# Low weight parts of the third group's block products: a ScalarE negation and an accumulating DMA in place of a VectorE subtraction, for six loads of fourteen

## The chip, the cores and the metric

The kernel runs on one core of a Trainium2 chip. A core has TensorE (PE, matrix products; its weight loads are shown apart as PEld), VectorE (DVE), ScalarE (ACT), GpSimd (POOL) and SyncE (SP), all running side by side, each working through its own list of instructions in order. DMAs move data between main memory and the on-chip memory SBUF; here SP issues the plain loads and POOL the accumulating ones, which add what they read to what lies at the destination. Matrix products land in PSUM, from which DVE or ACT take them away ("eviction"). The metric is the device time in microseconds of the whole program; lower is better.

## The reference, cut to what matters

The program is an encoder with two layers. Each layer is half a feed-forward block, a mixer (gated linear attention and softmax attention in parallel), and another half feed-forward block, on 528 tokens (512 and 16 learned ones) of 1024 channels, all in float32:

```python
for l in range(DEPTH):
    h = h + 0.5 * swiglu(rmsnorm(h, norm_gains[l, 0]), ffn_w_gate[l, 0], ffn_w_up[l, 0], ffn_w_down[l, 0])
    h = h + mixer(rmsnorm(h, norm_gains[l, 1]), ...)
    h = h + 0.5 * swiglu(rmsnorm(h, norm_gains[l, 2]), ffn_w_gate[l, 1], ffn_w_up[l, 1], ffn_w_down[l, 1])

def swiglu(x, w_gate, w_up, w_down):
    return (jax.nn.silu(x @ w_gate) * (x @ w_up)) @ w_down
```

The hidden width of a feed-forward block is 2816. The change lies in the last product, `... @ w_down`, of the first feed-forward block of each layer.

## The kernel before

**Numbers in two parts.** TensorE reads its operands in a shortened form of float32. To keep the accuracy, every weight tile `w` and every activation is split in two: a high part `hi`, which is `w` rounded to that form, and a low part `lo = w - hi`. A product then takes three matmuls: hi with the activation's high part, hi with its low part, and lo with the high part, in this order, so the low weight part is read by the third matmul of each three.

**Block products.** The feed-forward blocks use a two by two block scheme with seven products in place of eight. A product named "1" to "7" uses a block of the weight matrix or a sum of blocks. Products 1, 2 and 4 use plain blocks (11, 12 and 22, from `DIRECT`), which SP loads into the pool `raw` of three buffers (pool `wraw`). Products 7, 6, 5 and 3 use sums (`s3`, `s2`, `s1`, `s4`), most of them made by accumulating DMAs on POOL (`add`, line 224).

**Groups and steps.** The 22 hidden tiles are taken as 11 pairs in three groups of 4, 4 and 3 pairs (`GROUPS`). After each group its part of the down projection follows: for the two halves of the output ("quads", dq 0 and 1) seven products each, so fourteen loads a group. For the third group they are 768 columns wide, for the others 1024 (`wide`). Only the blocks in `ALL_FAST`, that is (0, 0) and (1, 0), take the third group in this way, so the program has two such stages of fourteen loads. I write a load as quad/product: 1/2 is product 2 of quad 1. `ffn_steps` writes the order by hand. In the third group it is: 0/1 (two pairs of three), product 4 of the last gate and up pair, 0/5 and 0/2 (two pairs of three each), then the third pair of 0/1, 0/5 and 0/2, and then `CLOSING`: 1/1, 0/6, 1/2, 0/7, 0/3, 0/4, 1/5, 1/6, 1/7, 1/3, 1/4. A whole product has 18 matmuls (three pairs, two column tiles, three matmuls); `fast_down` (line 745) issues them and adds the result to `h` (line 753).

**Making weights.** `Weights.make` takes the next load: ScalarE copies `w` to `hi` (line 310), VectorE subtracts to `lo` (line 311). The pools `whi` and `wlo` have four buffers each, so a `hi` can only be written once the oldest product that still holds a buffer has been worked off on TensorE. `use` asks for three loads ahead of the product in hand (`AHEAD_MADE - 1`). `fetch` starts the plain loads up to nine ahead. Where a load's raw tile is needed again for a sum, `sums` uses it: for the third group, `s4` is already made by ScalarE's negation of block 12 (`kept`, line 277) and an accumulating DMA of block 6's tile (`add`, line 224), and `s3` by ScalarE's negation (line 219) and an accumulating DMA from main memory; `s3` is then added to `s2` by another.

**What sets the order.** Dependencies and semaphores come from the framework, which also lays down each engine's list when the program is built: in the main the program's order, but an instruction whose inputs it expects late can be put behind later ones. On the chip each list runs in order. VectorE's list in this stage also holds the evictions (line 753), the low parts and differences of the activations (lines 701, 706, 710), and then the mixer's operands (lines 517, 526, 592).

Of the kernel before, what the change touches and what calls it, by code (L numbers as in the profile page):

```python
# [10 lines left out]
F32 = mybir.dt.float32  # L11
F32R = mybir.dt.float32r
U32 = mybir.dt.uint32
AF = mybir.ActivationFunctionType
ALU = mybir.AluOpType
# [17 lines left out]
SLAB = 1024  # L33
# [149 lines left out]
def wide(i):  # L183
    return SLAB if i < NPAIR else 2 * P * GROUPS[(i - NPAIR) // QUADS]


class Weights:
# [107 lines left out]
    def make(self, upto):  # L295
        nc = self.nc
        while self.made < min(upto, len(self.loads)):
            self.fetch(self.made + 1)
            s = self.made
            load = self.loads[s]  # L300
            w = self.raws.pop(s, None)
            if w is None:
                w = self.summed.pop(load)
            hi = self.hi_pool.tile([P, SLAB], F32R, tag="whi", name=f"whi{s}")
            lo = self.lo_pool.tile([P, SLAB], F32R, tag="wlo", name=f"wlo{s}")
            n = SLAB if isinstance(load, int) else wide(load[1])
            for a in np.split(np.arange(n), 2 if s == 0 else 1):
                cs = slice(a[0], a[-1] + 1)
                with self.tc.issue_after(self.behind) if self.behind else nullcontext():
                    nc.scalar.copy(hi[:, cs], w[:, cs])  # L310
                nc.vector.tensor_tensor(lo[:, cs], w[:, cs], hi[:, cs].bitcast(F32), ALU.subtract)  # L311
            self.got[s] = (hi, lo)
            self.got.pop(s - 12, None)
            self.made += 1
            if not isinstance(load, int) and load[2] in "126":
                self.sums(*load, w)
            after = self.loads[s + 1] if s + 1 < len(self.loads) else 0
            if not isinstance(after, int) and after[2] == "6" and after[1] < NPAIR and not self.chained(*after[:2]):
                s2, s3 = [self.summed[after[:2] + (c,)] for c in "67"]
                nc.vector.tensor_tensor(s2, s2, s3, ALU.add)  # L320
# [1113 lines left out]
```

## Time and profile before

| | |
|---|---|
| median of three runs | 2187.77 us (2187.23 to 2188.65) |
| the profiled execution: its time | 2187.4 us |
| the profiled execution: its span | 2185.6 us |
| mean granted TensorE clock | 0.999 |
| ScalarE busy | 57% of the span |
| GpSimd busy | 5% of the span |
| main memory read | 294.65 MB |

The span runs from the first to the last recorded instruction; 1.8 us of the execution lie around it. An engine's busy time is a sum over the span and says nothing of a single stage, so the stage is read from views cut to it: the first third-group stage runs from about 326 to 362 us of the span, the second from about 1420 to 1457 us. Rows of a timeline give start, duration, engine, line, operation, output<-input and, in brackets, the idle time before it and what ended it. `whi` and `wlo` are the two weight parts, `ss` is a PSUM accumulator, `g` and `c` are activation buffers, `win` is the weight array in main memory, and `s` and `w` are the tiles in which the block sums are made.

### The profile page before, as it was taken

To read this page: it belongs to the slowest core of one execution; us is meant where nothing else is said; L and a number is where in the kernel's file an instruction comes from. 1 tells how busy PE (TensorE), PEld (TensorE's weight loads), DVE (VectorE), ACT (ScalarE), POOL (GpSimd) and SP (SyncE) were. 2 spreads that over 40 slices of the span, in tenths; PEclk is the share of its full clock that TensorE was granted. 3 is DMA by queue.
4 is the path that set the end of the run, shared out by engine and by line. 5 is a ranking of instruction groups with operands and counts; after the bars stand their busy time and mean duration, and the time that the engine had idled before them with its cause. 6 is when DMAs were issued, how large, how long until landed. Compare 5 with 4: busy or idle time off the path is not lost.

```text
span 2185.6 us, 40161 instructions
## 1 busy us (share of the span) xinstructions
PE 2149.1 (98%) x16434; PEld 2056.1 (94%) x16434; DVE 1802.6 (82%) x2751; ACT 1245.9 (57%) x1844; POOL 119.0 (5%) x140
## 2 busy tenths in 40 slices
PE   7999999999999999999999999999999999999998
PEld 7999999989999999999999999988788888999997
DVE  8887979776976689888789979797779767997986
ACT  8545556444784556454575455574557836554544
POOL 1100000000000000010010000000000001000100
PEclk9999999999999999999999999999999999999999
DMA  9866755212113467676567667553121146775751
GB/s 286 218 195 182 202 154 139 82 51 76 49 40 123 130 177 180 202 185 183 167 162 187 199 181 204 153 140 97 49 78 49 49 135 152 199 204 178 196 162 68
DMA packets 91223, 320.32 MB, mean 147 GB/s; under 512 B 10144, under 2 KB 12576, under 8 KB 91040
## 3 DMA queue, kind: packets, MB, share of 16 engines
q1 hardware_dynamic: 70048, 246.58, 33.9%
q0 software_dynamic: 19584, 69.21, 17.6%
q8 instruction: 129, 2.11, 0.4%
q10 hardware_dynamic: 1408, 1.97, 0.3%
q14 instruction: 54, 0.44, 0.1%
HBM read 294.65 MB, written 2.10 MB: 136 GB/s over the span
## 4 chain that ended last, share of the span: by engine, by line
PE 83%; DVE 9%; ACT 4%; DMA 2%; issue 2%; SPq 0%; DVEq 0%; ACTq 0%
PE ss L621 36%; PE mm L488 15%; PE ss L745 14%; PE ss L488 7%; DVE wlo L311 3%; PE sm L488 2%; DMA w<-win 2%; PE sm L1125 1%; PE ss L1100 1%; ACT whi L310 1%; PE ss L494 1%; DVE h L753 1%; PE sm L1141 1%; PE ss L1101 1%; PE sm L1142 1%
## 5 line engine op out<-in xcount | busy, mean ns | idle before, releaser
L621 PE MATMUL ss<-xc,whi 128*128 128x264 f32 (+1 forms) x4928 | 903.1, 285 | 11.3 <-ACT whi L310 7.4
L621 PEld LDWEIGHTS ss<-xc,whi 128*128 128x128 f32 x4928 | 764.5, 189 | 14.9 <-ACT whi L310 8.0
L621 PE MATMUL ss<-xc,wlo 128*128 128x264 f32 (+1 forms) x2464 | 700.6, 285 | 4.0 <-DVE wlo L311 4.0
L311 DVE TENSOR_TENSOR wlo<-w,whi 128x1024 fp32r<-128x1024 f32 (+2 forms) x355 | 423.7, 1200 | 66.7 <-ACT whi L310 66.3
L621 PEld LDWEIGHTS ss<-xc,wlo 128*128 128x128 f32 x2464 | 465.0, 189 | 5.9 <-DVE wlo L311 5.9
L310 ACT CAST whi<-w 128x1024 fp32r<-128x1024 f32 (+2 forms) x355 | 362.1, 1036 | 169.3 <-PE ss L621 80.1
L488 PE MATMUL mm<-x,whi 128*128 128x264 f32 (+1 forms) x1712 | 385.5, 315 | 0.0
L488 PEld LDWEIGHTS mm<-x,whi 128*128 128x128 f32 x1712 | 278.1, 188 | 16.3 <-issue 1.0
L745 PE MATMUL ss<-g,whi 128*128 128x264 f32 (+1 forms) x1520 | 284.3, 285 | 3.6 <-DVE h L753 1.7
L488 PE MATMUL mm<-x,wlo 128*128 128x264 f32 (+1 forms) x856 | 266.3, 316 | 0.0
L745 PEld LDWEIGHTS ss<-g,whi 128*128 128x128 f32 x1520 | 236.2, 188 | 7.5 <-DVE g L706 3.6
L745 PE MATMUL ss<-g,wlo 128*128 128x264 f32 (+1 forms) x760 | 215.2, 283 | 0.0
L625 ACT COPY c<-ss 128x528 f32<-128x528 f32 (+1 forms) x132 | 78.4, 594 | 239.0 <-PE ss L621 238.7
L310 ACT CAST whi<-raw 128x1024 fp32r<-128x1024 f32 x114 | 119.3, 1048 | 130.7 <-PE mm L488 94.2
L311 DVE TENSOR_TENSOR wlo<-raw,whi 128x1024 fp32r<-128x1024 f32 x114 | 139.0, 1220 | 57.2 <-ACT whi L310 53.2
L488 PEld LDWEIGHTS mm<-x,wlo 128*128 128x128 f32 x856 | 159.6, 188 | 8.5 <-issue 0.5
L745 PEld LDWEIGHTS ss<-g,wlo 128*128 128x128 f32 x760 | 143.0, 188 | 0.0
L224 POOL DMA_DIRECT2D w<-win x64 | 56.1, 876 | 1453.2 <-DVE t L1261 342.0
L745 PE MATMUL ss<-c,whi 128*128 128x264 f32 (+1 forms) x608 | 115.5, 285 | 0.3
L311 DVE TENSOR_TENSOR wlo<-s,whi 128x1024 fp32r<-128x1024 f32 (+1 forms) x94 | 112.2, 1195 | 1.6 <-ACT whi L310 1.4
L467 ACT ACTIVATE c<-c 128x528 f32<-128x528 f32 (+1 forms) x88 | 56.5, 642 | 98.5 <-DVE c L671 98.4
L488 PE MATMUL ss<-g,whi 128*128 128x264 f32 (+2 forms) x516 | 103.6, 310 | 0.0
(270 smaller groups left out, 3379.1 us busy)
## 6 DMA issues: line engine op xcount, KB each, us to landing
w<-win SPq DMA_DIRECT2D x333, 512.0 KB, 4.4
raw<-wts SPq DMA_DIRECT2D x114, 512.0 KB, 3.3
w<-win POOLq DMA_DIRECT2D x60, 512.0 KB, 7.5
s<-win POOLq DMA_DIRECT2D x26, 512.0 KB, 7.5
w<-s POOLq DMA_DIRECT2D x26, 512.0 KB, 6.1
w<-win SPq DMA_DIRECT2D x20, 384.0 KB, 3.6
s<-w POOLq DMA_DIRECT2D x8, 512.0 KB, 7.4
h<-xt SPq DMA_DIRECT2D x3, 528.0 KB, 6.0
```

The lines of the kernel that those rows point to most:

```text
L224: self.nc.gpsimd.dma_start(t, src, accum_op=ALU.add)
L310: nc.scalar.copy(hi[:, cs], w[:, cs])
L311: nc.vector.tensor_tensor(lo[:, cs], w[:, cs], hi[:, cs].bitcast(F32), ALU.subtract)
L467: prev_act[0] = S.activation(*args, **kw).ins
L488: TE.matmul(acc.half[i][:width], lhs, rhs[:, acc.spans[i]], start=first, stop=last)
L494: TE.matmul(a, weights, x[:, hs], start=True, stop=True)
L621: TE.matmul(acc[:, j], a[:, j, k], b[:, at], start=bool(begin and k == 0 and i == 0), stop=k == len(x) - 1 and i == 2, skip_group_check=no ...
L625: W.behind = S.copy(part(st, q), acc).ins
L745: closing[0] = TE.matmul(acc[:, j], a[:, j, k], xs[b][:, k], start=bool(begin and k == 0 and i == 0), stop=k == n - 1 and i == 2, skip_gro ...
L753: V.tensor_tensor(to, to, acc, ALU.add)
L1100: TE.matmul(s[:n, i, :HF], lhs, kh[:, hs], start=True, stop=False)
L1101: TE.matmul(s[:n, i, :HF], lhs, kl[:, hs], start=False, stop=True)
```

## The change

For loads narrower than 1024 columns, so those of the third group alone, the low part of products 2, 7 and 4 is no longer subtracted by VectorE. ScalarE writes the negated high part into `lo`, and POOL issues a DMA that adds `w`, from SBUF, to it. These are the loads 0/2, 1/2, 0/7, 0/4, 1/7 and 1/4 of each of the two stages: twelve in the program. The other eight of a stage, and all wider loads, stay as they were.

```diff
                 with self.tc.issue_after(self.behind) if self.behind else nullcontext():
                     nc.scalar.copy(hi[:, cs], w[:, cs])
-                nc.vector.tensor_tensor(lo[:, cs], w[:, cs], hi[:, cs].bitcast(F32), ALU.subtract)
+                if not isinstance(load, int) and wide(load[1]) < SLAB and load[2] in "274":
+                    nc.scalar.activation(lo[:, cs], hi[:, cs].bitcast(F32), AF.Copy, scale=-1.0)
+                    self.add(lo[:, cs].bitcast(F32), w[:, cs])
+                else:
+                    nc.vector.tensor_tensor(lo[:, cs], w[:, cs], hi[:, cs].bitcast(F32), ALU.subtract)
```

`add` is the accumulating DMA that the sums use:

```python
    def add(self, t, src):

        self.nc.gpsimd.dma_start(t, src, accum_op=ALU.add)
```

## The prediction

> **What bounds the kernel now.** I read the busy times of the page first, then the busy times cut to the two stages of the change, then what TensorE waited for there, and last the timelines of ScalarE, TensorE and GpSimd.
>
> ```profile
> PE 2149.1 (98%) x16434; PEld 2056.1 (94%) x16434; DVE 1802.6 (82%) x2751; ACT 1245.9 (57%) x1844; POOL 119.0 (5%) x140
> ```
>
> Over the whole span TensorE is the bound, at 98%. In the two stages VectorE is as full:
>
> ```profile
> core 0: us, PE busy (x) PEld busy (x) DVE busy (x) ACT busy (x) POOL busy (x), PEclk, DMA share, GB/s
> 326.00:362.00 36.00, 34.68 (x277) 33.70 (x276) 35.03 (x53) 24.88 (x35) 4.39 (x5) 1.00 0.65 169
> 1420.00:1456.00 36.00, 34.73 (x278) 33.92 (x277) 35.26 (x53) 24.40 (x35) 4.38 (x5) 1.00 0.67 174
> PE ss L745 <- DVE h L753: 0.9, 2, 0.6
> PE ss L745 <- DVE g L706: 0.4, 1, 0.4
> ```
>
> The first two rows are the stages, with busy times and instruction counts in the order of the heading; the last two are TensorE's own waits from 326 to 362 us (in total, times, longest). VectorE is busy for 35.0 of 36 us, and TensorE loses 36.00 - 34.68 = 1.3 us, which the waits put down to VectorE: two evictions (0.9) and one activation part (0.4). So VectorE is a second bound of this stage, but what it costs is small: 1.3 us here and 36.00 - 34.73 = 1.3 in the other, 2.6 in all. By the weight loads, the stricter count, it is 2.3 + 2.1 = 4.4. No relief of VectorE in these stages can give more than that. Behind the stage, from 362 to 420 us, the waits name none of TensorE at all, so VectorE's saved time is worth nothing there.
>
> **What goes.** Six subtractions leave VectorE in each stage:
>
> ```profile
> L311 DVE TENSOR_TENSOR wlo<-w,whi 128x768 fp32r<-128x768 f32 x20 | 19.0, 951 | 0.2
> L277 ACT ACTIVATE s<-w x4: 827/838/845, 328.3 to 1437.0; 128x768 f32<-128x768 f32 x4
> ```
>
> The first row is the subtraction at 951 ns, 5.7 us of VectorE a stage. The second is the nearest thing to what comes in: ScalarE's negation of a 768 wide tile (shortest, median and longest in ns), 838 ns, 5.0 us a stage. ScalarE is busy for 24.9 of 36 us, so it has room for the sum; what counts is where the negation stands in the chain.
>
> **What comes in is a longer chain.** Before, `lo` was ready about a subtraction after `hi`. Now it is `hi`, the negation, GpSimd's issue, and a DMA that reads SBUF and adds to SBUF. The lead is the time from the start of `hi` to the third matmul of the product, the first to read `lo`. ScalarE's side:
>
> ```profile
> 326.29 0.83 ACT L310 CAST whi<-w 128x768 fp32r<-128x768 f32 x1 [2.08 <-PE ss L621]
> 334.33 1.57 ACT L310 CAST whi<-w 128x768 fp32r<-128x768 f32 x2 [0.41 <-PE ss L745]
> 336.12 0.83 ACT L310 CAST whi<-s 128x768 fp32r<-128x768 f32 x1
> 340.49 0.83 ACT L310 CAST whi<-w 128x768 fp32r<-128x768 f32 x1 [0.64 <-PE ss L745]
> 348.57 0.83 ACT L310 CAST whi<-s 128x768 fp32r<-128x768 f32 x1
> 353.27 0.83 ACT L310 CAST whi<-w 128x768 fp32r<-128x768 f32 x1 [1.35 <-PE ss L745]
> ```
>
> These are `hi` of 0/2; of 0/6 and 1/2 in one row; of 0/7, 0/4, 1/7 and 1/4. Four of the six waited for TensorE ("<-PE"): a `hi` starts when a product gives its buffer back, so a lead can't be stretched by starting earlier. TensorE's side, the first matmul on `lo` of the same six:
>
> ```profile
> 332.29 0.29 PE L745 MATMUL ss<-g,wlo 128*128 128x264 f32 x1
> 340.65 0.28 PE L745 MATMUL ss<-g,wlo 128*128 128x264 f32 x1
> 343.50 0.28 PE L745 MATMUL ss<-g,wlo 128*128 128x264 f32 x1
> 349.02 0.28 PE L745 MATMUL ss<-g,wlo 128*128 128x264 f32 x1
> 355.33 0.28 PE L745 MATMUL ss<-g,wlo 128*128 128x264 f32 x1
> 360.51 0.28 PE L745 MATMUL ss<-g,wlo 128*128 128x264 f32 x1
> ```
>
> The second `hi` of the pair starts 0.74 after the first, at 335.07, because two back to back take 1.57. The leads are then 6.0 (0/2), 5.6 (1/2), 7.4 (0/7), 8.5 (0/4), 6.8 (1/7) and 7.2 us (1/4). The second stage has the same build; its first `hi` and first use are
>
> ```profile
> 1420.97 0.84 ACT L310 CAST whi<-w 128x768 fp32r<-128x768 f32 x1 [2.08 <-PE ss L621]
> 1426.96 0.28 PE L745 MATMUL ss<-g,wlo 128*128 128x264 f32 x1
> ```
>
> again a lead of 6.0, so I double the first stage's sum. `hi` and the negation take 1.57 together, as the pair does; I add 0.1 for the hand to GpSimd, an estimate from its rows, which start within some tenths of what they wait for. The DMA, from issue to landing, may then take 6.0 - 1.7 = 4.3 us for 0/2, 3.9 for 1/2, 5.7 for 0/7, 6.8 for 0/4, 5.1 for 1/7 and 5.5 for 1/4. What accumulating DMAs of this size took in the stage, by their issues (one row each, cut to 318 to 319, 328.5 to 329.5, 329.5 to 330.5, 336.9 to 337.5 and 343.7 to 344.5 us; the last but one column is their size, the last us to landing):
>
> ```profile
> w<-s POOLq DMA_DIRECT2D x1, 384.0 KB, 3.8
> ...
> s<-win POOLq DMA_DIRECT2D x1, 384.0 KB, 7.5
> ...
> s<-w POOLq DMA_DIRECT2D x1, 384.0 KB, 8.9
> ...
> w<-s POOLq DMA_DIRECT2D x1, 384.0 KB, 6.0
> ...
> s<-w POOLq DMA_DIRECT2D x1, 384.0 KB, 5.0
> ```
>
> The time follows the traffic: between 328 and 338 us loads and accumulates share the DMA engines, later there are few. A new DMA is priced by the row nearest to its issue. For 0/2, issued at about 326.29 + 1.7 = 328.0, that is the 7.5 of 328.8, and it is 7.5 - 4.3 = 3.2 us late. For 1/2, issued some 3 us after 336.8 by then, it is the 6.0 of 336.97: 6.0 - 3.9 = 2.1 late. Its lead isn't helped by the first stall: its buffer comes from 0/5, whose third pair stands behind 0/2 in TensorE's list, so both ends of the lead move. For 0/7, 6.0 - 5.7 = 0.3, but its `hi` takes 0/2's buffer, released before 1/2 stalls, so it gains 2.1 and is in time; so is 0/4. For 1/7 and 1/4 the row is the 5.0 of 343.76: in time by 0.1 and 0.5. A stage stalls 3.2 + 2.1 = 5.3 us.
>
> While TensorE waits, VectorE catches up, so the 1.3 us that it cost go: 5.3 - 1.3 = 4.0 us a stage, 8.0 in both. Queued behind TensorE's wait are all later matmuls, and behind those the buffers of later loads, so a stall here isn't made good: the mixer's first products follow the last of this stage.
>
> [...]
>
> **What is costed at nothing.** GpSimd has 31 us free in a stage, and an issue takes about 0.87; its own waits:
>
> ```profile
> 328.83 0.86 POOL L224 DMA_DIRECT2D s<-win  x1 [9.64 <-DVE c L671]
> 336.97 0.87 POOL L224 DMA_DIRECT2D w<-s  x1 [4.95 <-issue]
> ```
>
> An issue placed behind the second of these would wait for it; 0/2 is ready at 328.0, ahead of the first, and the others after 337. Moving `s<-win` back by one issue delays sums that are needed after 340 us. The raw buffer of 0/2 is held until its DMA has landed at about 335.5, and the load of 0/4 with it, but that one is needed at 340.5 plus the stall: hidden, about 1 us if it were not.
>
> **Bounds.** Lowest: every DMA at 3.8 us: nothing is late, and VectorE's cost goes, -2.6 to -4.4. Highest: 8.9 us for 0/2 and 1/2 and 6.0 for 1/7: 4.6 + 5.0 + 0.9 - 1.3 = 9.2 a stage, +18.4. The sum is made on the profiled execution: 2187.4 + 8.0 = 2195.4 us; that execution lies 0.4 below the median, so the forecast stands for the median within 0.4.
>
> **The rivals.**
>
> *The lists are laid anew around the late parts.* While 0/2 waits, 0/1 and 0/5 have six matmuls left each and 1/1 has 18; at 34.68 / 277 = 0.125 us each that is 3.8 us, enough for the 3.2. For it: the framework does move matmuls, as the row
>
> ```profile
> 342.60 0.28 PE L745 MATMUL ss<-g,whi 128*128 128x264 f32 x1
> ```
>
> shows, a single matmul of a later product ahead of 0/7. Against it: it moved one, not a product, and it needs an estimate as long as the chip's 7.5 us. Then only 1/2's 2.1 stays or goes: (2.1 - 1.3) or -1.3 a stage, 2189.0 to 2184.8, say 2187.
>
> *The other side: the low parts land in time.* If the DMAs take less than 3.9 us, the tightest slack, nothing stalls and the 2.6 to 4.4 us come back: 2184.8 to 2183.0, say 2184. For it the 3.8 at 318.3, against it the four later rows. [...]
>
> *More traffic, more lateness.* Six more accumulates meet the same DMA engines from 328 to 345 us and each takes the 8.9 of its neighbour: 2200 to 2206, say 2203.
>
> That the change isn't in force isn't one: the condition names twelve loads.
>
> **How the numbers follow.** Forecast 0.46, ranging from 2190 to 2200 (a microsecond more or less on each of four stalls); lists laid anew 0.22; in time 0.12; more traffic 0.20. About 0.2%, 4.4 us, is what can be told from no change, so faster is below 2183.4 and slower above 2192.1. Faster: half of the third case, 0.06. Same: its other half, 0.20 of the second and 0.05 of the forecast, 0.31. Slower: 0.63. The range 2184.5 to 2205 leaves out about half of the in-time case and half of the traffic case's upper end.
>
> **What would show it.** TensorE's waits in the two stages name a DMA onto `wlo` at 0/2 and 1/2, 2 to 4 us each, and hardly at 0/4 and 1/4; VectorE's idle time there grows to some 10 us; the accumulates `lo<-w` land in 5 to 9 us. Rather wrong: TensorE as busy as before in both stages, matmuls of 1/1 ahead of 0/2's low part, or landings under 4 us.

## The result and the profile after

The changed kernel takes 2201.09 us (median of four executions, 2200.53 to 2204.1) beside 2187.5 us of the kernel before (2186.79 to 2188.65): a ratio of 1.0064, 95% interval 1.0051 to 1.0076, so 0.0064 x 2187.5 = 14.0 us slower by the ratio (11.2 to 16.6). The forecast was 2195.4 us, the range 2184.5 to 2205. The profiled execution is the longest of the four, 2204.1 us with a span of 2202.2, 16.6 more than the span before; what follows accounts for those 16.6, and the losses of the experiments, in us, are their ratios less 1 times 2187.5. In the code, lines behind the change stand four further down: the subtraction is L315, the block products' matmul L749, the eviction L757; the new negation is L312.

First the page's row of busy times, then the two stages, 36 us of each (columns as in the prediction):

```profile
PE 2153.5 (98%) x16434; PEld 2060.1 (94%) x16434; DVE 1794.7 (81%) x2739; ACT 1255.3 (57%) x1856; POOL 129.4 (6%) x152
326.00:362.00 36.00, 29.93 (x240) 29.11 (x240) 27.21 (x43) 25.55 (x37) 8.74 (x10) 1.00 0.85 193
1428.00:1464.00 36.00, 29.58 (x228) 29.15 (x227) 24.35 (x38) 22.05 (x32) 8.72 (x10) 0.95 0.87 193
```

The first row shows little: twelve instructions have moved from VectorE to ScalarE (2751 to 2739, 1844 to 1856) and twelve DMAs have come to GpSimd. The stages show it. In the first, TensorE works 29.93 of 36 us and gets through 240 matmuls where it did 277; VectorE is down from 35.0 to 27.2, so it has the 8.8 us of idle time that the prediction put at some 10. In the second the granted clock, the column before the DMA share, is 0.95 and no longer 1.00.

What TensorE waited for, from 318 to 380 us and then from 1410 to 1480 us (in total, times, longest):

```profile
PE ss L749 <- DMA wlo<-w: 5.2, 2, 3.2
PE ss L749 <- DVE h L757: 1.0, 2, 0.7
PE ss L749 <- ACT whi L310: 0.9, 1, 0.9
...
PE ss L749 <- DMA wlo<-w: 6.4, 2, 3.2
PE ss L749 <- ACT whi L310: 1.5, 1, 1.5
PE ss L749 <- DVE h L757: 1.0, 2, 0.7
```

Two new waits on a low part in each stage, 5.2 and 6.4 us; and other waits, put down to a high part and to evictions, 1.9 and 2.5, where the kernel before had 1.3 in each. The timeline of TensorE says where they stand:

```profile
336.35 0.39 PE L749 MATMUL ss<-g,wlo 128*128 128x264 f32 x1 [3.20 <-DMA wlo<-w]
346.60 0.39 PE L749 MATMUL ss<-g,wlo 128*128 128x264 f32 x1 [1.98 <-DMA wlo<-w]
360.95 0.48 PE L749 MATMUL ss<-g,whi 128*128 128x264 f32 x2 [0.87 <-ACT whi L310]
...
1438.74 0.39 PE L749 MATMUL ss<-g,wlo 128*128 128x264 f32 x1 [3.22 <-DMA wlo<-w]
1450.25 0.39 PE L749 MATMUL ss<-g,wlo 128*128 128x264 f32 x1 [3.20 <-DMA wlo<-w]
```

These are the first matmuls on the low parts of 0/2 and 1/2, in both stages, and at the end of the first stage the first matmul of 1/3, the product that needs the sum `s4` of quad 1. That row names a high part, but by the times it was an eviction that 1/3 waited for: its own `hi` had ended at 358.52, the eviction of 1/5, whose accumulator it adds to, ended at 360.81, and the `hi` that ended at 360.94 is that of 1/4. The low parts of 0/7, 0/4, 1/7 and 1/4 were in time.

The 16.6 us of span by place, each from the starts of a stage's first matmul and of the mixer's first matmul behind it, in the timelines of both kernels:

| | before | after | longer by |
|---|---|---|---|
| up to the first stage | 326.22 | 326.92 | 0.7 |
| first stage | 36.24 | 42.18 | 5.9 |
| between the stages | 1058.43 | 1060.18 | 1.8 |
| second stage | 36.04 | 45.31 | 9.3 |
| behind the second stage | 728.67 | 727.61 | -1.1 |

The first stage's 5.9 are its waits: 5.2 + 1.9, less the 1.3 lost before, is 5.8. The second stage's are 6.4 + 2.5 - 1.3 = 7.6, and 1.7 of the 9.3 are missing. Here are two microsecond windows around the end of its second stall (columns as above, the clock third from the end):

```profile
1448.00:1450.00 2.00, 0.00 (x0) 0.00 (x0) 1.13 (x2) 1.99 (x3) 0.00 (x0) 1.00 0.95 181
1450.00:1452.00 2.00, 1.75 (x9) 1.75 (x10) 0.73 (x1) 1.07 (x2) 0.52 (x1) 0.68 0.10 18
1452.00:1454.00 2.00, 2.00 (x11) 2.00 (x10) 0.19 (x1) 0.41 (x1) 0.34 (x1) 0.50 0.62 121
1454.00:1456.00 2.00, 2.00 (x17) 2.00 (x17) 2.00 (x3) 1.98 (x4) 0.42 (x1) 0.97 0.40 75
...
564.00:566.00 2.00, 2.00 (x11) 1.93 (x11) 1.10 (x3) 0.48 (x2) 0.00 (x0) 0.50 0.00 0
```

After the stall TensorE is busy without a gap and yet does 11 matmuls in 2 us instead of 17: its clock was granted at half. Half clock for the time t costs t/2, and the clock column gives t: 2 x 2.00 x (0.32 + 0.50 + 0.03) = 3.4 us, so 1.7 us are lost, the missing ones. The stall ahead of them is 3.20 us long; the stalls at 0/2, 3.20 and 3.22 us, have no half clock behind them. The last row is another such stretch, in the mixer of the first layer between the stages, with no wait near it; it is the 1.8 of the table.

So 11.6 us are the two low parts (10.6 were forecast), 4.4 - 2.6 = 1.8 the waits that should have gone and grew, and 3.4 two stretches at half clock: 16.8, less the 0.4 of the table's first and last rows, is 16.4 against 16.6.

**Where the landings stood.** Rows of the view of DMA issues, cut to one issue each: 0/2, 1/2, 0/7, 0/4, 1/7 and 1/4 of the first stage.

```profile
wlo<-w POOLq DMA_DIRECT2D x1, 384.0 KB, 6.2
wlo<-w POOLq DMA_DIRECT2D x1, 384.0 KB, 5.1
wlo<-s POOLq DMA_DIRECT2D x1, 384.0 KB, 5.3
wlo<-w POOLq DMA_DIRECT2D x1, 384.0 KB, 3.8
wlo<-s POOLq DMA_DIRECT2D x1, 384.0 KB, 4.2
wlo<-w POOLq DMA_DIRECT2D x1, 384.0 KB, 3.9
```

All are shorter than the rows by which they were priced. Why 0/2 was late all the same, and why the sums came late, stands on the lists of ScalarE and GpSimd. The timeline of ScalarE after, then that of GpSimd:

```profile
327.00 0.84 ACT L310 CAST whi<-w 128x768 fp32r<-128x768 f32 x1 [2.09 <-PE ss L625]
328.83 0.83 ACT L312 ACTIVATE wlo<-whi 128x768 fp32r<-128x768 f32 x1
330.10 0.83 ACT L277 ACTIVATE s<-w 128x768 f32<-128x768 f32 x1
349.47 0.84 ACT L277 ACTIVATE s<-w 128x768 f32<-128x768 f32 x1
357.68 0.84 ACT L310 CAST whi<-s 128x768 fp32r<-128x768 f32 x1 [2.83 <-DMA s<-w]
```

```profile
329.33 0.86 POOL L224 DMA_DIRECT2D s<-win  x1 [10.40 <-DVE c L675]
330.06 1.05 POOL L224 DMA_DIRECT2D wlo<-w  x1
334.97 0.87 POOL L224 DMA_DIRECT2D w<-s  x1 [2.24 <-issue]
336.62 0.86 POOL L224 DMA_DIRECT2D s<-w  x1 [0.78 <-issue]
350.72 0.86 POOL L224 DMA_DIRECT2D s<-w  x1 [2.01 <-DVE g L705]
```

and the same two sums in GpSimd's timeline before, with the negation that the second waits for in ScalarE's:

```profile
329.56 1.04 POOL L224 DMA_DIRECT2D s<-w  x1
343.76 0.87 POOL L224 DMA_DIRECT2D s<-w  x1 [5.92 <-ACT s L277]
342.51 0.84 ACT L277 ACTIVATE s<-w 128x768 f32<-128x768 f32 x1 [0.42 <-DVE wlo L311]
```

`s<-w` are the accumulates that finish `s4`, of quad 0 and then of quad 1. Both are some 7 us later. Of this, 0.7 us for quad 0 and some 5 us for quad 1 are the shift of the whole schedule (TensorE gets to 1/3 at 355.09 before and at 360.08 after), so about 6 and 2 us are lateness of their own. For quad 0 the reason is the order: 0/2's negation (328.83) stands on ScalarE where the negation for `s4` stood, that one moves to 330.10, and GpSimd's list now has this sum behind `w<-s`, which waits for `s<-win`. Before, it stood ahead. `hi` of 0/3, which reads this sum, then waits for it (0.93 us in the first stage, 2.17 in the second), but no wait of TensorE follows from that here. For quad 1 the lists laid down when the programs are built show a changed wait. The negation for that `s4`, before and then after, with its place on ScalarE's list:

```
264 L277 ACTIVATE s_00_16_4089<-w_00_16_3756 128x768 [waits DVE_49]
269 L277 ACTIVATE s_00_16_4093<-w_00_16_3756 128x768 [waits DMASW2_49]
```

It waited for VectorE; now it waits for a DMA, and by its place in the queue that is 0/7's accumulate. Its tile is a buffer that 0/7's sum `s3` had, and that is free only when the DMA which reads it has landed, 343.10 + 5.3 = 348.4 us, not when VectorE has subtracted (342.48 before). The framework also put the negation behind the `hi` of 1/5, which waits until 1/2 is worked off (348.73). So `s4` of quad 1 is issued at 350.72, takes 6.9, `hi` of 1/3 starts at 357.68 (before: 351.08), VectorE's subtraction waits for it, the evictions of 1/5 and 1/6 stand behind that on VectorE, and TensorE waits for the first at 360.95 and for the second at 363.06.

### The profile page after: what moved, and what is told of

Its sections match the earlier page's. It is cut to its first block, busy times and chain, and to the rows that moved or that the text cites. A ratio compares the mean times of both kernels' runs of the same rounds, so it can differ in the third digit from the quotient of the medians.

```text
span 2202.2 us, 40197 instructions
## 1 busy us (share of the span) xinstructions
PE 2153.5 (98%) x16434; PEld 2060.1 (94%) x16434; DVE 1794.7 (81%) x2739; ACT 1255.3 (57%) x1856; POOL 129.4 (6%) x152
## 4 chain that ended last, share of the span: by engine, by line
PE 82%; DVE 8%; ACT 4%; DMA 4%; issue 3%; SPq 0%; POOL 0%; DVEq 0%; ACTq 0%; POOLq 0%
PE ss L625 36%; PE mm L492 15%; PE ss L749 14%; PE ss L492 8%; PE sm L492 2%; DVE wlo L315 2%; PE sm L1129 1%; DMA wlo<-w 1%; PE ss L1104 1%; PE ss L498 1%; ACT whi L310 1%; PE sm L1145 1%; PE ss L1105 1%; DMA w<-win 1%; PE sm L1146 1%
## 5 line engine op out<-in xcount | busy, mean ns | idle before, releaser
L625 PE MATMUL ss<-xc,whi 128*128 128x264 f32 (+1 forms) x4928 | 903.8, 285 | 11.6 <-ACT whi L310 7.3
L315 DVE TENSOR_TENSOR wlo<-w,whi 128x1024 fp32r<-128x1024 f32 (+2 forms) x347 | 417.5, 1210 | 71.2 <-ACT whi L310 70.9
L749 PE MATMUL ss<-g,whi 128*128 128x264 f32 (+1 forms) x1520 | 284.7, 285 | 5.4 <-ACT whi L310 2.4
L749 PEld LDWEIGHTS ss<-g,whi 128*128 128x128 f32 x1520 | 237.2, 189 | 8.5 <-ACT t L526 2.7
L749 PE MATMUL ss<-g,wlo 128*128 128x264 f32 (+1 forms) x760 | 216.3, 285 | 11.6 <-DMA wlo<-w 11.6
L315 DVE TENSOR_TENSOR wlo<-raw,whi 128x1024 fp32r<-128x1024 f32 x114 | 139.3, 1222 | 59.3 <-ACT whi L310 55.2
L749 PEld LDWEIGHTS ss<-g,wlo 128*128 128x128 f32 x760 | 143.7, 189 | 12.4 <-DMA wlo<-w 12.4
L749 PE MATMUL ss<-c,whi 128*128 128x264 f32 (+1 forms) x608 | 115.7, 285 | 0.4
L315 DVE TENSOR_TENSOR wlo<-s,whi 128x1024 fp32r<-128x1024 f32 (+1 forms) x90 | 108.9, 1210 | 7.2 <-ACT whi L310 6.9
L757 DVE TENSOR_TENSOR h<-h,ss 128x528 f32<-128x528 f32 (+1 forms) x140 | 96.6, 700 | 11.5 <-PE ss L749 11.1
```

The lines of the kernel that those rows point to most:

```text
L625: TE.matmul(acc[:, j], a[:, j, k], b[:, at], start=bool(begin and k == 0 and i == 0), stop=k == len(x) - 1 and i == 2, skip_group_check=no ...
L749: closing[0] = TE.matmul(acc[:, j], a[:, j, k], xs[b][:, k], start=bool(begin and k == 0 and i == 0), stop=k == n - 1 and i == 2, skip_gro ...
L757: V.tensor_tensor(to, to, acc, ALU.add)
```

## The experiments

Each is an edit of the changed kernel; where only the condition differs, only that is shown. The times are medians beside the kernel before on the same chip, in brackets the 95% interval of the ratio. "Stage" is by how much the two stages of the profiled execution are longer than before, as in the table above. My theory at the outset was that the lateness of 0/2 and 1/2 makes the loss and that the waits at the stage's end follow from sums that come later; the rivals were that ScalarE's negations or the DMAs as such make it.

**1. The negation without the DMA.**

```diff
                     nc.scalar.activation(lo[:, cs], hi[:, cs].bitcast(F32), AF.Copy, scale=-1.0)
-                    self.add(lo[:, cs].bitcast(F32), w[:, cs])
```

> The change without its accumulating DMAs: for the twelve loads the low part is only the negated high part, so w is left out of it. VectorE is relieved and ScalarE has its twelve negations, but no DMA is waited for. Theory (the landing of the DMA costs, not ScalarE's work): TensorE waits on no DMA in the two stages, and the 2.6 to 4.4 us that VectorE cost come back: 2183 to 2186 us, ratio 0.998 to 0.9995. Rival (ScalarE's longer list delays what stands behind the negations): above 2190.

2192.52 us (1.0012 to 1.0029), stage +1.5 and +2.7: missed, the rival held. The six negations a stage, without a DMA, cost 4.4 of the 14.0 us where a gain was expected. From its GpSimd and ScalarE timelines:

```profile
335.13 1.15 POOL L224 DMA_DIRECT2D s<-w  x1
342.94 0.83 ACT L310 CAST whi<-s 128x768 fp32r<-128x768 f32 x1 [3.15 <-DMA s<-w]
```

The sum `s4` of quad 0 is again issued behind `w<-s`, and `hi` of 0/3 waits 3.15 us for it. So the displaced sum comes with the negation and needs no accumulate on a low part. In the profile, 1.7 us of the second stage are lost at half clock.

**2. Without 0/2 and 1/2**, the two that were late.

```diff
-... and load[2] in "274":
+... and load[2] in "74":
```

> Products 0/2 and 1/2 back on VectorE; 0/7, 0/4, 1/7 and 1/4 stay on the DMA. Theory (lead against landing time, load by load): the two long waits of each stage go; 0/7 has lost the slack that the wait at 1/2 gave it and may be up to 1 us late: 2186 to 2191 us. Rival (each accumulate costs about the same, 13.6 / 12 = 1.1 us): 8 x 1.1 = +9, 2196.

2192.2 us (1.0009 to 1.0028), stage +3.1 and +2.0: missed by 1.2 us, but well under the rival. TensorE now waits 2.0 and 2.1 for 0/7, which was in time in the changed kernel, 0.85 for 1/4 in the first stage, and half clock follows both of the longer stalls. 0/7's accumulate took 4.1 us, less than the 5.7 that it had by the prediction, but its `hi` and its negation are no longer back to back. ScalarE's timeline:

```profile
336.92 0.84 ACT L310 CAST whi<-s 128x768 fp32r<-128x768 f32 x1
339.11 0.86 ACT L707 CAST g<-g 128x792 fp32r<-128x792 f32 x1 [1.35 <-PE ss L749]
340.61 0.84 ACT L312 ACTIVATE wlo<-whi 128x768 fp32r<-128x768 f32 x1
```

Between them the list has a cast of an activation that waits for TensorE (and `hi` of 0/3): 3.7 us from start to start in place of the 0.74 that I had priced. `s4` of quad 0 is back in its old place in GpSimd's list.

**3. Without 0/7**, whose DMA holds the buffer that `s4` of quad 1 takes.

```diff
-... and load[2] in "274":
+... and load[2] in "274" and load[1:] != (15, "7"):
```

> Load 0/7 alone back on VectorE. Its DMA was never waited for by TensorE. Theory (the s3 tile of 0/7 is held until that DMA has landed, the s4 tile of quad 1 takes its buffer, so s4, its high part and VectorE's list behind it come late at the end of the stage): the last three waits of the stage (1.9 and 2.5 us in the two stages) fall to at most the 0.6 of before, the waits on the DMA at 0/2 and 1/2 stay: 2195 to 2198.5 us. Rival (those last waits come from the shift of the schedule or from ScalarE): within 1.2 us of the change, 2200 to 2202.

2204.92 us (1.0062 to 1.0088), stage +10.2 and +6.5: the time missed by far. The mechanism held: the negation for `s4` of quad 1 waits for VectorE again in the built list, and the waits at the stage's end fall from 1.9 and 2.5 to 0.5 and 0.8. But that negation now stands ahead of 0/4's on ScalarE, and so does its DMA on GpSimd. From GpSimd's timeline, the view of issues and TensorE's timeline:

```profile
349.86 0.87 POOL L224 DMA_DIRECT2D s<-w  x1 [5.20 <-ACT s L277]
350.59 1.02 POOL L224 DMA_DIRECT2D wlo<-w  x1
wlo<-w POOLq DMA_DIRECT2D x1, 384.0 KB, 7.9
358.50 0.39 PE L749 MATMUL ss<-g,wlo 128*128 128x264 f32 x1 [3.29 <-DMA wlo<-w]
```

The last row is 0/4: two transfers issued 0.73 us apart take 6.7 and 7.9 us in the first stage, where 0/4's took 3.8 in the changed kernel, and a stall is given back at 0/4 (0.69 in the second stage). The profile also has five times 3.41 us at half clock, 1.7 us lost each time, where the changed kernel's has two.

**4. Without 1/7**, the same for the other quad.

```diff
-... and load[2] in "274":
+... and load[2] in "274" and load[1:] != (16, "7"):
```

> Load 1/7 alone back on VectorE, the counterpart of the run without 0/7: as many accumulates fewer, but its s3 tile is waited for by no sum of the stage. Theory: all waits stay, 2200 to 2202 us. Rival (each accumulate costs about 1.1 us): 2198.9 for two fewer, and the same in both runs.

2205.11 us (1.0064 to 1.0089), stage +6.2 and +7.2: the waits stay, as expected, but the time is 3 us over the range. No gain: the negation still waits for 0/7's DMA, and the DMA waits are 4.5 and 5.5. The waits at the stage's end are 1.2 and 0.9, less than in the changed kernel, but behind the stage TensorE now waits 1.6 and 1.5 for an operand of the mixer.

**5. VectorE's relief alone**: 0/7, 0/4, 1/7 and 1/4 negated, no DMA.

```diff
-... and load[2] in "274":
+... and load[2] in "74":
                     nc.scalar.activation(lo[:, cs], hi[:, cs].bitcast(F32), AF.Copy, scale=-1.0)
-                    self.add(lo[:, cs].bitcast(F32), w[:, cs])
```

> Negation without the accumulating DMA, for 0/7, 0/4, 1/7 and 1/4 only; w is left out of those eight low parts. 0/2 and 1/2 stay on VectorE, so GpSimd's list is that of before (s4 of quad 0 ahead of the sum for quad 1). Theory (what made the run without DMAs slow is 0/2's negation, which pushes s4 of quad 0 behind that sum): TensorE's waits in the stages fall to 1.3 us or less each, 2184.5 to 2188 us. Rival (ScalarE's extra work itself costs): above 2190, as with all twelve.

2185.17 us (0.9980 to 0.9997), stage -0.9 and -0.9: as expected. This is the price of VectorE as a second bound, 2.4 us (0.7 to 4.4 by the interval), just under the 2.6 to 4.4 that the prediction allowed. `s4` of quad 0 is issued at 330.03, in its old place.

**6. The other two negations alone**, 0/2 and 1/2.

```diff
-... and load[2] in "274":
+... and load[2] in "2":
                     nc.scalar.activation(lo[:, cs], hi[:, cs].bitcast(F32), AF.Copy, scale=-1.0)
-                    self.add(lo[:, cs].bitcast(F32), w[:, cs])
```

> The counterpart: negation without the DMA for 0/2 and 1/2 only, w left out of those four low parts. Theory (the displaced s4): waits on ScalarE and on the activation part of product 3 as with all twelve, about 2.5 to 3 us a stage, 2190 to 2193.5 us. Rival (ScalarE's extra work, by its amount): a third of the 4.4 us of all twelve, 2189.5 or less.

2188.75 us (0.9996 to 1.0014), stage +0.3 and +2.0: under the expected loss and within the rival's 2189.5, not told apart from no change. `s4` of quad 0 is late (334.74), but alone that makes only small waits, 1.5 us in the first stage and 2.2, with half clock behind them, in the second. With experiment 5 the first one is explained only in part: -2.4 and +1.1 don't add up to +4.4, so some of that loss comes with all six negations together. One difference shows on ScalarE: in experiment 1 the negation for `s4` of quad 1 runs ahead of product 3's activation (343.68 and 344.43), here behind it (344.76 and 343.99). Whether that is the whole of it was not tested.

**7. Only 0/4 and 1/4**, the two with the longest leads.

```diff
-... and load[2] in "274":
+... and load[2] in "4":
```

> The change for 0/4 and 1/4 alone, the loads with leads of 8.5 and 7.2 us; nothing left out. Theory (lead against landing time): both land in time, VectorE is relieved of four subtractions, 2185 to 2188.5 us. Rival (each accumulate costs 1.1 us): 2192.5.

2195.64 us (1.0020 to 1.0045), stage +4.0 and +3.0: missed, a loss where a gain was expected, and over the rival's 2192.5. From ScalarE's and TensorE's timelines (the last row is ScalarE again):

```profile
341.33 0.84 ACT L310 CAST whi<-w 128x768 fp32r<-128x768 f32 x1 [0.66 <-PE ss L749]
344.10 0.83 ACT L312 ACTIVATE wlo<-whi 128x768 fp32r<-128x768 f32 x1
351.53 0.39 PE L749 MATMUL ss<-g,wlo 128*128 128x264 f32 x1 [1.51 <-DMA wlo<-w]
...
367.87 1.05 ACT L310 CAST whi<-raw 128x1024 fp32r<-128x1024 f32 x1 [3.51 <-DMA raw<-wts]
```

`hi` of 0/4 and its negation start 2.8 us apart, not 0.74: an activation cast (L704) and the negation for `s4` stand between them. The DMA goes out at 345.33, behind `s4`'s at 344.60, and lands 6.2 us later, 1.5 too late. Half clock follows in both stages, 1.7 us each, and 1/4 is 0.8 late in the first. And the raw buffer of 1/4 is held until its DMA has landed, so the load that takes it next comes late: ScalarE waits 3.51 for it, and the mixer's operand behind it on ScalarE makes TensorE wait 1.65.

**8. Four late products**, 0/4, 1/5, 1/6 and 1/4, with 0/2 and 0/7 as before.

```diff
-... and load[2] in "274":
+... and load[1:] in ((15, "4"), (16, "5"), (16, "6"), (16, "4")):
```

> Four loads of each stage that have long leads, 0/4, 1/5, 1/6 and 1/4 (8.5, 8.0, 7.5, 7.2 us), take the negation and the DMA, the others VectorE; nothing left out. Theory: as many accumulates as without product 2, but none is waited for long, 2184 to 2189 us. Rival (each accumulate costs 1.1 us): 2197.

2197.66 us (1.0033 to 1.0060), stage +5.0 and +5.7: missed. From GpSimd's and TensorE's timelines:

```profile
348.99 0.87 POOL L224 DMA_DIRECT2D wlo<-w  x1 [0.57 <-ACT wlo L312]
351.54 0.51 PE L749 MATMUL ss<-c,whi 128*128 128x264 f32 x2 [0.17 <-DVE h L757]
355.60 0.46 PE L749 MATMUL ss<-c,wlo 128*128 128x264 f32 x1 [3.55 <-DMA wlo<-w]
356.95 0.42 PE L749 MATMUL ss<-g,whi 128*128 128x264 f32 x1
```

One stall of 3.5 us in each stage, at 1/5, and half clock behind it. These loads were chosen by their leads in the timeline before, and the lead of 1/5 was no longer there: in the list built for this kernel the framework put its first eight matmuls ahead of all but one of 0/4's eighteen (in the rows, activation `c` is 1/5's and `g` 0/4's), where before all of them stood behind 0/4. Its accumulate, the third of four sums and low parts issued from 346.64 to 352.13, took 6.6 us and landed at 355.55. That of 1/6, issued last, was in time.

**9. The changed kernel again.**

> The changed kernel once more, for more executions and a second profile beside the runs of this call. Theory: 2200 to 2204 us; the waits at 0/2 and 1/2 in both stages within 1 us of the first profile's 3.2 and 2.0 to 3.2; the executions with the lower mean granted clock are the longer ones, by some 1.7 us for each 0.0008 of the clock (3.4 us at half clock).

2201.2 us (1.0053 to 1.0078), stage +5.8 and +9.3. The same to 0.1 us, as expected, but not stall by stall: the wait at 1/2 in the first stage is off by more than the 1 us allowed. The relation of clock and time did not show either: the longest of the five executions (2204.33 us) has a mean clock of 0.996, and none of the others has a higher one. TensorE's timeline in the first stage and the window behind its first stall:

```profile
336.86 0.39 PE L749 MATMUL ss<-g,wlo 128*128 128x264 f32 x1 [3.11 <-DMA wlo<-w]
347.38 0.39 PE L749 MATMUL ss<-g,wlo 128*128 128x264 f32 x1 [0.73 <-DMA wlo<-w]
...
338.00:340.00 2.00, 2.00 (x12) 2.00 (x12) 0.00 (x0) 0.58 (x1) 0.00 (x0) 0.57 1.07 201
```

A stall of 3.11 us now brings half clock, where 3.20 in the first profile did not; TensorE is slower behind it, 1/2's DMA lands in 4.3 us instead of 5.1, and so it is only 0.73 late, not 1.98. Clock and stall partly stand in for each other.

**10. Only 0/2 and 1/2**, the two late ones by themselves.

```diff
-... and load[2] in "274":
+... and load[2] in "2":
```

> The change for 0/2 and 1/2 alone, nothing left out. Theory (those two loads make most of the loss): the DMA waits stay at 5 to 6.5 us a stage, the waits at the end of the stage are no more than the 0.6 of before (0/7 holds nothing), 2196.5 to 2200 us. Rival (each accumulate costs 1.1 us): a third of the loss, 2192.

2197.27 us (1.0035 to 1.0060), stage +4.4 and +5.0: the time as expected, the waits on the DMA not. They are 3.8 and 2.7 us, under the 5 to 6.5: behind the first stall TensorE runs at half clock, for 3.4 and 6.8 us (1.7 and 3.4 lost), and 1/2 is then 0.8 late and not late at all. The waits at the stage's end are 0.8 and 0.8, not 1.9 and 2.5, and the negation for `s4` of quad 1 waits for VectorE. The two late parts, with the half clock behind them, make 10.5 of the 14.0 us; the rest comes only with the other four.

**11. GpSimd subtracts** for 0/7, 0/4, 1/7 and 1/4, without negation or DMA; nothing is left out.

```diff
-... and load[2] in "274":
-                    nc.scalar.activation(lo[:, cs], hi[:, cs].bitcast(F32), AF.Copy, scale=-1.0)
-                    self.add(lo[:, cs].bitcast(F32), w[:, cs])
+... and load[2] in "74":
+                    nc.gpsimd.tensor_tensor(lo[:, cs], w[:, cs], hi[:, cs].bitcast(F32), ALU.subtract)
```

> 0/7, 0/4, 1/7 and 1/4 take the subtraction on GpSimd itself (one tensor operation, w minus high part), no negation and no DMA; nothing left out. Theory (the relief of VectorE is worth the 2.4 us that the run with those four negations showed, and only the landing time spoiled it): in time with leads of 6.8 us and more if the operation takes under 4 us, 2184 to 2187 us. Rival (GpSimd's operation slows VectorE, or stands in its list behind a DMA's wait): 2188 or more.

2193.61 us (1.0016 to 1.0036), stage +2.4 and +4.4: missed, the rival held. From GpSimd's timeline and VectorE's:

```profile
343.96 1.85 POOL L312 TENSOR_TENSOR wlo<-w,whi 128x768 fp32r<-128x768 f32 x1 [2.30 <-ACT whi L310]
344.70 1.93 DVE L314 TENSOR_TENSOR wlo<-s,whi 128x768 fp32r<-128x768 f32 x1
```

The subtraction takes GpSimd 1.85 us (1.83 to 2.54 for the eight) where VectorE takes 0.95, and VectorE's own subtraction that starts within it takes 1.93. GpSimd is done 1.11 us after VectorE's start, and 1.11 + 0.95 = 2.06, near the 1.93: by these two rows VectorE hardly gets on until then. TensorE waits 3.4 and 3.9 us in the two stages instead of 1.3, all of it for VectorE: 2.1 a stage for evictions, the rest for activation parts.

No version that computes the whole was faster than the kernel before.

## Why the prediction held, and where its steps failed

**The two late low parts: right in place, and in size partly by luck.** 3.2 and 2.1 us a stage were forecast for 0/2 and 1/2; 3.20 and 1.98 were measured in the first stage, 3.22 and 3.20 in the second, and no wait on the other four. Experiment 10 shows that with the half clock behind them they cost 10.5 us by themselves. For 0/2 two errors cancelled. The 1.7 us from `hi` to the issue were 1.3 too short: it went out 3.06 us after `hi` (327.00 to 330.06), because the negation for `s3`, itself held 0.24 us by a load, runs on ScalarE between the two, and because the hand to GpSimd takes 0.40 us from the end of the negation, for all twelve low parts, not 0.1. And the price of 7.5 us was 1.3 too long; it took 6.2. 1/2 is alike: issued 2.3 us after `hi`, landed in 5.1 in the first stage, not 6.0, and in 6.3 in the second.

**VectorE's 1.3 us a stage: not given back.** "While TensorE waits, VectorE catches up, so the 1.3 us that it cost go" is the term that was wrong: the waits grew to 1.9 and 2.5 us, so 1.8 were lost where 2.6 were to be won. VectorE did get its room; experiment 5 shows what that is worth, 2.4 us. But what held the stage's end was no longer the amount of VectorE's work, it was a sum that ScalarE and VectorE waited for, with the evictions behind it.

**What was costed at nothing.** This is the step behind it. "Moving `s<-win` back by one issue delays sums that are needed after 340 us" looked at the issue and not at the order. 0/2's negation and DMA took the places of `s4`'s on two in-order lists, and that sum fell behind one that waits. Eleven timelines of GpSimd agree: the sum is issued behind `w<-s`, at 334.7 to 336.9, in the six kernels that have 0/2's negation (the changed one and experiments 1, 3, 4, 6 and 10, of which 1 and 6 add no DMA), and right behind `s<-win`, at 330.0 to 332.5, in the five that haven't (2, 5, 7, 8 and 11). In the changed kernel that late sum makes no wait of TensorE; the one of quad 1 does. And the prediction counted the raw buffer that the DMA holds, not the block sum: 0/7's `lo` is made from `s3`, whose buffer the next `s4` takes. Taking 0/7's accumulate away (experiments 3 and 10) brought the wait back to VectorE and the waits at the end of the stage down to 0.5 to 0.8 (1.2 and 0.9 in experiment 4, which keeps it, but with the waits on the mixer behind them). Experiment 2 keeps 0/7's accumulate and has no such wait, but there the framework gave that `s4` another buffer, that of quad 0's `s4`. What held the negation last was its place behind `hi` of 1/5: in the first stage the DMA's landing and the start of that `hi` lie 0.3 us apart (348.41 and 348.73), in the second 1.5 us (1452.06 and 1453.59), and in both the negation starts right behind the `hi` (349.47 and 1454.33). That the wait for the DMA is why the framework put it there is argued from experiments 3 and 10, where it stands ahead of that `hi`; more buffers for that pool were not tried.

**Leads read off the old timeline.** "`hi` and the negation take 1.57 together, as the pair does" held for 0/7 and 1/7 here. For 1/2, 0/4 and 1/4 the two start 1.05 to 1.5 us apart, not 0.74, for 0/2 1.83, and where the lists came out otherwise it is more: 3.7 us in experiment 2 and 2.8 in experiment 7, each with a stall of 1.5 to 2.1 us that the old lead rules out. So "in time" was right for the other four in this kernel, and not for 0/7 in experiment 2, 0/4 in 3 and 7, 1/4 in 2, 4 and 7 or 1/5 in 8. One lead was misread, without effect: in the list built for the kernel before, twelve of 1/3's matmuls stand ahead of 1/7, so the row at 355.33 is 1/3's, 1/7 first reads its low part at 356.78, and its lead is 8.2 us, not 6.8.

**The clock: not foreseen.** Half clock for 3.4 us behind a stall costs 1.7 us. Leaving out the first and the last 25 us of the span, the changed kernel's two profiles have two and three such stretches, the kernel before none. The length of a stall alone does not tell whether one follows (3.11 with, 3.20 without). The stretches of a profile start whole multiples of 3.41 us apart; in the first profile they start at 563.24 and 1450.71, 887.47 us or 260 times 3.4133 apart, and in experiment 3's timeline of TensorE the slow matmuls end at 342.56 and 363.06, 20.50 us or six times 3.417 apart. Laid out in pieces of 3.41 us from these starts, the first profile's stalls without half clock are split, 1.4 + 1.8 and 1.5 + 1.7 us, and the one with it lies almost whole in a piece, 2.96; in the second profile the 3.11 us are 1.1 + 2.0. In the thirteen profiles, each of the 17 pieces in which TensorE stood idle for 1.89 us or more was followed by half clock; of the 22 with 1.5 to 1.85 us four were; with less idle time none was but those near 564 us. A stretch near 564 us, with no wait ahead of it, stands in eight of the thirteen profiles and not in the kernel before; its cause stays open. Nor is it known why the profiled execution of the changed kernel lies 3 us above the others, at the same mean clock within 0.001.

**The rivals.** *Lists laid anew around the late parts* fell for TensorE at 0/2 and 1/2, where it waited in its old order; on ScalarE and GpSimd the lists were laid anew, to the change's cost and not to its relief. The argument against it, that the framework moves single matmuls, was too strong: it had moved twelve of 1/3's already before, and in experiment 8 it moved eight of 1/5's. *In time* fell for 0/2 and 1/2; three of six landings in the first stage are 3.8 to 4.2 us (0/4, 1/7 and 1/4), but none of these had another accumulate beside it for its whole way, 0/4 for 1.5 of 3.8 us, 1/7 for 2.4 of 4.2 and 1/4 not at all. *More traffic* came nearest in time, 2203, and was wrong in its mechanism: the low parts landed in 3.8 to 6.6 us, not 8.9. The sum was short mostly by what follows from order, buffers and clock (4.4 and 3.4 us), and by 1.0 through the DMAs. The price for each accumulate isn't a constant either: it is 0.5 us each in experiment 2 (eight), 1.2 in the changed kernel (twelve), 1.3 in experiment 8 (eight) and 1.8 in experiment 7 (four).

## What to carry to other kernels

An engine's operation that is replaced by a DMA costs the time from issue to landing in that very stage (3.8 to 6.6 us here), held against the lead of what reads it; and it holds its source until it lands (0/7's sum here until 348.4, where VectorE had subtracted at 342.48 before), so ask who takes that buffer next. A lead read off the old timeline holds only if the new instructions displace nothing on lists that run in order: write down, for each list, what stood where the new instruction will stand and who waits for that. A stall can cost 1.7 us more at half clock; in these thirteen profiles 1.9 us of idle TensorE within one piece of 3.41 us, counted from the start of a half-clock stretch, were always followed by it.

## What was not expected of the hardware

- The same accumulate of 384 KB from SBUF to SBUF took 3.8 us at its shortest, with the DMA engines busy for 58% of its first 2.9 us (0/4 here), and 6.2 to 7.9 where another had been issued 0.7 us before it (0/2 here at 6.2, 0/4 in experiments 3 and 7 at 7.9 and 6.2).
- TensorE was put to half clock for 3.4 or 6.8 us after stalls as short as 1.5 us (experiment 7, 351.53), and not after two of 3.2 us in the changed kernel; and once in eight of the thirteen profiles, the changed kernel's two among them, with no stall near.
- A GpSimd subtraction of two tiles doubled the time of a VectorE subtraction that ran into it, 0.95 to 1.93 us.
